# Ordering a two-layer sequence trunk by the tile scheduler's finer simulation

## The chip, the cores and the metric

The kernel runs on one core of one Trainium2 chip. The metric is the device time of one execution in microseconds. Engines are named as in the profile: PE is TensorE's matmul side, PEld its weight loads, DVE is VectorE, ACT is ScalarE, POOL is GpSimd, SP is SyncE, which here only issues DMAs.

## The reference

A sequence of 256 positions of width 1024 goes through two layers. Each layer is a half-step SwiGLU feed-forward block (FFN, inner width 2816), a mixer, and a second FFN, each with an RMS norm ahead of it and behind it and a residual addition:

```python
for i in range(DEPTH):          # 2
    x = x + 0.5 * rms_norm(swiglu(rms_norm(x, g[0]), ffn_wgu[i, 0], ffn_wd[i, 0]), g[1])
    h = rms_norm(x, g[2])
    mix = diff_rwkv_mixer(h, ...) if i % 2 == 0 else retention_mixer(h, ...)
    x = x + rms_norm(mix, g[3])
    x = x + 0.5 * rms_norm(swiglu(rms_norm(x, g[4]), ffn_wgu[i, 1], ffn_wd[i, 1]), g[5])
```

The even layer's mixer runs differential attention (4 heads) beside an RWKV-7 recurrence (8 heads of 64), both behind one input projection and ahead of one output projection. The odd layer's mixer is retention (4 heads) in matrix form. All data are float32.

## The kernel before

The 256 positions are two blocks of 128, b=0 and b=1. The plan is six sub-layers: FFN, even mixer, FFN, FFN, odd mixer, FFN. Every weight is used once by both blocks and is streamed from DRAM: `pump` (L279 to L302) issues one 512 KB DMA per half unit on SP into one of 3 `raw` buffers, then ACT rounds it to float32r (`wh`, L299) and DVE takes the rest (`wl`, L300); 8 buffers hold each of `wh` and `wl`. A product is the sum of three float32r matmuls (high by high, high by low, low by high): `proj` (L315 to L317), `outp` (L327 to L329), `proj_features` (L340 to L342). In most chunks of an FFN both blocks share one weight load in `proj_parts` (L354, L355), and `joined` (L363 and L364) adds the two halves out of PSUM on ACT and DVE, behind which come the SwiGLU steps (L528 to L535) and `outp`.

A sub-layer ends in `post` (L464 to L471: sum of squares on ACT, the inverse root on POOL, the residual addition into `x` on DVE), and the next begins with `pre` (eight transposes on PE, L418, turned into `xp` by ACT and DVE, L423 and L424). One block's hand-over from `post` to `pre` is a chain, beside which PE can only run what the other block still has.

In the even mixer, `rwkv` (one job per block, lanes 0 and 2) and `attention` (lane 1) are generators that are stepped between the units of the projections. The recurrence is solved by doubling: five levels, each a group of small matmuls (L1122), a mask on DVE (L1125), a second group (L1129), and DVE additions and transposes (L1131, L1133), each needing the one before it. PSUM has four tags of two banks: `mm`, `tp`, `ac0`, `ac1`.

All instructions are written into one block by Python; `run` (L1267) fixes the order in which the two blocks, the weight pump and the lanes are written. The order in which each engine gets them is the tile scheduler's: it simulates the program while it orders it, and hands each engine, of the instructions whose inputs and buffers are ready in the simulation, the one of highest priority. Priority is the order of writing, lifted in the hand-overs (`LIFT_PRE, LIFT_POST = 300, 100`) and in the lanes (`LIFT = (200, 600, 600)`), by that many instructions. Each engine then runs its instructions in the order given, and an instruction that waits holds up those behind it on its engine.

## Time and profile before

| | |
|---|---|
| median of 3 runs | 1206.8 us (1206.78 to 1227.89) |
| profiled execution | 1209.15 us |
| its span, first to last instruction | 1207.4 us |
| mean granted TensorE clock | 0.993 |
| PE busy | 1178.7 us |
| DVE, ACT busy | 756.6, 629.1 us |
| read from DRAM | 197.50 MB, 164 GB/s |

The span is shorter than the execution by what lies before the first and behind the last instruction, 1.75 us. Busy times are of the profiled execution; a matmul's end is modelled, so a stretch in which PE is shown busy throughout can hold short pauses.

### The profile page before, as it was taken

What the parts mean: (1) busy time and instruction counts of PE and PEld (TensorE: products, weight loads), DVE (VectorE), ACT (ScalarE), POOL (GpSimd) and SP (SyncE); (2) the same over time, 40 slices, a digit from 0 to 9 for tenths busy, and PEclk for the clock granted to TensorE, in tenths of its full rate; (3) what the DMA queues carried; (4) which work ended last, traced back from release to release, by engine and by line L of the source; (5) the groups of instructions that cost most, each with busy time, mean ns of one, the idle gap of its engine ahead of it and who ended that gap; (6) DMA issues with size and microseconds to landing.
All of it is one profiled execution on the core that took longest, in us unless ns stands there. A gap on an engine that the chain in (4) does not pass through costs nothing.

```text
span 1207.4 us, 17468 instructions
## 1 busy us (share of the span) xinstructions
PE 1178.7 (98%) x6760; PEld 966.9 (80%) x6760; DVE 756.6 (63%) x1147; ACT 629.1 (52%) x1055; POOL 39.0 (3%) x53
## 2 busy tenths in 40 slices
PE   7999999999999999999999999999999999999997
PEld 5788887788777778888878888877877777888886
DVE  5666666687644766666676656575544457666663
ACT  6554555744452465455565555565434456555552
POOL 0000000000001100000010000010000001000000
PEclk9999999999989999999999999999999999999999
DMA  8655655442141256565546556555525555556551
GB/s 278 220 189 180 204 178 177 141 132 61 37 132 45 69 178 206 186 194 188 181 159 205 190 180 192 192 192 178 178 97 175 163 167 177 194 190 192 192 189 38
DMA packets 55412, 199.70 MB, mean 165 GB/s; under 512 B 6176, under 2 KB 6432, under 8 KB 55328
## 3 DMA queue, kind: packets, MB, share of 16 engines
q1 hardware_dynamic: 54576, 196.90, 50.3%
q8 instruction: 53, 0.87, 0.3%
q0 software_dynamic: 320, 1.05, 0.3%
q10 hardware_dynamic: 432, 0.63, 0.2%
q14 instruction: 31, 0.25, 0.1%
HBM read 197.50 MB, written 1.05 MB: 164 GB/s over the span
## 4 chain that ended last, share of the span: by engine, by line
PE 84%; DMA 5%; DVE 4%; ACT 3%; issue 2%; POOL 1%; SPq 0%; DVEq 0%; POOLq 0%; ACTq 0%
PE ps L354 24%; PE ps L355 12%; PE ps L329 8%; PE ps L327 8%; PE ps L328 8%; PE ps L315 5%; PE ps L317 4%; PE ps L316 4%; DMA raw<-in_wts_dram 4%; DVE wl L300 2%; ACT wh L299 2%; PE p L1122 1%; PE p L1129 1%; PE tp L418 1%; PE yp L603 1%
## 5 line engine op out<-in xcount | busy, mean ns | idle before, releaser
L300 DVE TENSOR_TENSOR wl<-raw,wh 128x1024 fp32r<-128x1024 f32 (+1 forms) x368 | 443.1, 1207 | 251.5 <-ACT wh L299 249.3
L299 ACT CAST wh<-raw 128x1024 fp32r<-128x1024 f32 (+1 forms) x368 | 380.5, 1037 | 254.6 <-PE ps L354 73.7
L354 PE MATMUL ps<-xp,wh 128*128 128x512 f32 x1312 | 469.7, 400 | 5.7 <-DVE sgh L513 2.0
L355 PE MATMUL ps<-xp,wl 128*128 128x256 f32 x1312 | 369.0, 281 | 0.0
L354 PEld LDWEIGHTS ps<-xp,wh 128*128 128x128 f32 x1312 | 247.3, 188 | 71.1 <-DVE gate L364 10.2
L355 PEld LDWEIGHTS ps<-xp,wl 128*128 128x128 f32 x1312 | 249.3, 190 | 1.5
L327 PE MATMUL ps<-wh,hx 128*128 128x512 f32 x448 | 178.3, 398 | 0.0
L328 PE MATMUL ps<-wl,hx 128*128 128x512 f32 x448 | 177.4, 396 | 0.0
L329 PE MATMUL ps<-wh,hx 128*128 128x512 f32 x448 | 177.3, 396 | 0.0
L315 PE MATMUL ps<-wh,xp 128*128 128x512 f32 (+1 forms) x320 | 130.8, 411 | 1.8 <-ACT xp L423 1.2
L316 PE MATMUL ps<-wl,xp 128*128 128x512 f32 (+1 forms) x320 | 127.0, 399 | 0.0
L317 PE MATMUL ps<-wh,xp 128*128 128x512 f32 (+1 forms) x320 | 126.0, 398 | 0.7 <-DVE xp L424 0.5
L329 PEld LDWEIGHTS ps<-wh,hx 128*128 128x128 f32 x448 | 84.1, 188 | 20.7 <-DVE hx L376 0.3
L327 PEld LDWEIGHTS ps<-wh,hx 128*128 128x128 f32 x448 | 84.1, 188 | 20.1 <-ACT hx L375 0.4
L328 PEld LDWEIGHTS ps<-wl,hx 128*128 128x128 f32 x448 | 84.2, 188 | 18.0
L315 PEld LDWEIGHTS ps<-wh,xp 128*128 128x128 f32 x320 | 61.0, 191 | 22.1 <-ACT xp L423 7.1
L317 PEld LDWEIGHTS ps<-wh,xp 128*128 128x128 f32 x320 | 61.0, 191 | 15.8 <-DVE xp L424 2.9
L363 ACT COPY gate<-ps 128x256 f32<-128x256 f32 x74 | 27.2, 368 | 86.0 <-PE ps L355 85.9
L316 PEld LDWEIGHTS ps<-wl,xp 128*128 128x128 f32 x320 | 61.0, 191 | 12.8 <-issue 1.9
L364 DVE TENSOR_TENSOR gate<-ps,gate 128x256 f32<-128x256 f32 x74 | 31.2, 421 | 57.0 <-ACT gate L363 57.0
L363 ACT COPY h<-ps 128x256 f32<-128x256 f32 x74 | 27.1, 367 | 50.1 <-PE ps L355 50.1
L424 DVE SCALAR_TENSOR_TENSOR xp<-tp,c,xp 128x128 fp32r<-128x128 f32 x96 | 30.6, 347 | 11.9 <-ACT xp L423 10.6
(241 smaller groups left out, 959.6 us busy)
## 6 DMA issues: line engine op xcount, KB each, us to landing
raw<-in_wts_dram SPq DMA_DIRECT2D x362, 512.0 KB, 4.4
gpost<-in_rows_dram SPq DMA_DIRECT2D x6, 512.0 KB, 5.6
x<-in_x_dram SPq DMA_DIRECT2D x4, 256.0 KB, 6.2
ups<-in_ups_dram SPq DMA_DIRECT2D x1, 768.0 KB, 5.8
ce<-in_ce_dram SPq DMA_DIRECT2D x1, 644.0 KB, 8.3
lnw<-in_rows_dram POOLq DMA_DIRECT2D x2, 256.0 KB, 4.1
lnb<-in_rows_dram POOLq DMA_DIRECT2D x2, 256.0 KB, 3.7
dec<-in_co_dram SPq DMA_DIRECT2D x1, 512.0 KB, 3.5
```

Of the source, the lines that this page charges most:

```text
L299: nc.scalar.copy(out=h[:, c], in_=r[:, c])
L300: nc.vector.tensor_tensor(out=l[:, c], in0=r[:, c], in1=h[:, c].bitcast(F32), op=ALU.subtract)
L315: mm(ps[:, :width], lhsT=xh[:, kt, :], rhs=h[:, c], start=first and i == 0, stop=False)
L316: mm(ps[:, :width], lhsT=xh[:, kt, :], rhs=l[:, c], start=False, stop=False)
L317: mm(ps[:, :width], lhsT=xl[:, kt, :], rhs=h[:, c], start=False, stop=last and i == n - 1)
L327: mm(acc[n], lhsT=hh[:, t], rhs=wh[:, c], start=first and t == 0, stop=False)
L328: mm(acc[n], lhsT=hh[:, t], rhs=wl[:, c], start=False, stop=False)
L329: mm(acc[n], lhsT=hl[:, t], rhs=wh[:, c], start=False, stop=last and t == 1)
L354: mm(ps, lhsT=h[:, c], rhs=both, start=kt == 0, stop=False)
L355: mm(ps[:, :256], lhsT=l[:, c], rhs=both[:, :256], start=False, stop=kt == 7)
L363: self.nc.scalar.copy(out=o, in_=ps[:, 256:])
L364: self.nc.vector.tensor_tensor(out=o, in0=ps[:, :256], in1=o, op=ALU.add)
```

## The change

The scheduler's simulation is exchanged: with the flag, the order is found on the library's timeline simulation, which keeps the sequencers, the queues in front of the engines, the DMA queues and the semaphores as parts with times of their own, in place of the coarser one. The instructions, their operands, the number of buffers and the priorities are the same; what can differ is the order of the instructions on each engine, which buffer of a tag a tile gets, and with these the waits between the engines.

```diff
-    with tile.TileContext(nc) as tc:
+    with tile.TileContext(nc, schedule_with_timeline_sim=True) as tc:
         trunk_body(tc, io, out)
```

## Rows read from the trace of the kernel before

**Rows 1.** The page's part 1, busy time, share, instructions of each engine.

```profile
PE 1178.7 (98%) x6760; PEld 966.9 (80%) x6760; DVE 756.6 (63%) x1147; ACT 629.1 (52%) x1055; POOL 39.0 (3%) x53
```

**Rows 2.** Busy time of each engine by stretch; columns in the first row.

```profile
core 0: us, PE busy (x) PEld busy (x) DVE busy (x) ACT busy (x) POOL busy (x), PEclk, DMA share, GB/s
0.00:60.00 60.00, 50.22 (x229) 40.07 (x230) 37.60 (x72) 37.30 (x70) 1.32 (x6) 0.94 0.76 250
60.00:200.00 140.00, 139.84 (x726) 117.94 (x725) 89.55 (x110) 73.17 (x100) 0.00 (x0) 1.00 0.58 188
200.00:450.00 250.00, 243.27 (x2083) 194.10 (x2082) 162.97 (x342) 123.28 (x282) 22.87 (x25) 0.99 0.31 101
450.00:600.00 150.00, 150.00 (x787) 126.73 (x786) 95.62 (x118) 79.45 (x111) 0.00 (x0) 1.00 0.60 191
600.00:640.00 40.00, 39.61 (x181) 31.11 (x180) 28.63 (x51) 25.53 (x52) 3.12 (x4) 1.00 0.51 169
640.00:790.00 150.00, 150.00 (x787) 126.75 (x786) 95.78 (x119) 79.51 (x111) 0.00 (x0) 1.00 0.59 190
790.00:850.00 60.00, 57.92 (x278) 46.34 (x278) 40.05 (x62) 37.40 (x65) 3.06 (x4) 1.00 0.58 188
850.00:1030.00 180.00, 177.41 (x830) 141.10 (x829) 100.07 (x143) 88.22 (x144) 7.52 (x12) 1.00 0.49 158
1030.00:1190.00 160.00, 160.00 (x830) 134.69 (x829) 99.96 (x124) 82.16 (x115) 0.00 (x0) 1.00 0.55 178
1190.00:1207.40 17.40, 10.47 (x45) 8.07 (x43) 6.38 (x11) 3.12 (x8) 1.10 (x2) 0.87 0.16 60
```

**Rows 3.** What PE waited for: us in total, times, longest us.

```profile
PE tp L418 <- DMA c<-in_c_dram: 4.2, 1, 4.2
PE tp L418 <- DVE x L471: 2.4, 6, 0.6
PE ps L354 <- DVE gate L364: 2.0, 2, 1.8
```

**Rows 4.** Stretches at TensorE's lower clock and one behind; columns as above.

```profile
25.40:28.80 3.40, 3.40 (x12) 2.81 (x12) 2.69 (x3) 1.50 (x3) 0.00 (x0) 0.50 0.94 338
52.70:56.10 3.40, 3.40 (x13) 2.91 (x12) 3.00 (x4) 1.58 (x2) 0.00 (x0) 0.50 0.78 235
349.70:356.50 6.80, 6.80 (x31) 5.45 (x30) 3.06 (x6) 2.08 (x4) 2.31 (x4) 0.50 0.21 77
356.50:366.00 9.50, 9.50 (x69) 6.49 (x70) 4.41 (x6) 4.90 (x11) 1.43 (x3) 1.00 0.42 140
```

**Rows 5.** Timeline, PE's two long waits in the start; [idle before, what ended it].

```profile
25.16 0.59 PE L354 MATMUL ps<-xp,wh 128*128 128x512 f32 x1 [2.05 <-DVE sgh L513]
...
51.93 0.50 PE L354 MATMUL ps<-xp,wh 128*128 128x512 f32 x1 [1.85 <-DVE gate L364]
```

**Rows 6.** Timeline, one level of the recurrence (start, length, engine, line, operation).

```profile
255.97 1.15 PE L1122 MATMUL p<-work 64*64 64x64 f32 x32
...
257.48 0.68 PE L1129 MATMUL p<-work 64*64 64x64 f32 x16
...
258.40 0.68 PE L1129 MATMUL p<-work 64*64 64x64 f32 x16
258.76 0.79 DVE L1131 TENSOR_TENSOR work<-p,work 128x256 f32<-128x256 f32 x2
...
259.47 0.76 DVE L1133 STREAM_TRANSPOSE work<-work 128x256 f32<-128x256 f32 x2
...
260.88 1.15 PE L1122 MATMUL p<-work 64*64 64x64 f32 x32
```

**Rows 7.** Timeline, block 0's hand-over at 202 us; [idle before, what ended it].

```profile
202.55 0.40 PE L329 MATMUL ps<-wh,hx 128*128 128x512 f32 x1
203.34 0.66 PE L418 MATMUL tp<-c,x 128*128 128x128 f32 x4 [0.39 <-DVE x L471]
```

**Rows 8.** Activation table loads at L512, a group of the lines: busy us, mean ns.

```profile
L512 ACT ACT_TABLE_LOAD x2 | 2.6, 1283 | 0.6 <-issue 0.6
```

## The prediction

> **What bounds the kernel now.** I read the page's shares first. PE is shown busy for 1178.7 of 1207.4 us, DVE and ACT for 63% and 52% [rows 1]. No DMA figure comes near a bound over a whole stretch: the DMA engines' share in the long FFN stretches is 0.55 to 0.60 [rows 2]. So the kernel is bound by PE, and a new order can't take away matmuls; it can only remove or add time in which PE has nothing that it may run, and time at the lower clock.
>
> Where that time lies is read from the stretches. The inner parts of the four FFNs (60 to 200, 450 to 600, 640 to 790 and 1030 to 1190 us, together 600 us) show PE busy for 599.84 us. The even mixer with its two edges, 200 to 450, lacks 250 - 243.27 = 6.73 us; the edge at 600 to 640 lacks 0.39, that at 790 to 850 2.08, the odd mixer 2.59. The start, 0 to 60, lacks 9.78 and the end, 1190 to 1207.4, 6.93 [rows 2]. The sum is 28.7 us, the difference between the span and PE's busy time.
>
> Of this some is out of reach of any order. At the start PE waits 4.2 us for the first constants to land [rows 3]. At the end the last block's norm and its output follow the last matmul, 6.93 us. That leaves 28.7 - 4.2 - 6.93 = 17.6 us in play.
>
> The clock is the second loss. Three stretches, 3.4, 3.4 and 6.8 us long, are granted 0.50, the lower of the two levels [rows 4]. The first two stand in the start-up, each just behind one of PE's two longest waits after the first (2.05 us for DVE's `sgh`, 1.85 us for `gate`) [rows 5]. The third stands in the even mixer, in a stretch that shows PE busy throughout, so being shown busy doesn't keep the clock. With half the rate in 13.6 us, the three cost some 6.8 us by an estimate from these rows. So the most that a perfect order could give back is 17.6 + 6.8 = 24.4 us, 2.0% of 1207.
>
> **The change part by part.** Nothing is computed more or less, so every term is a wait that comes or goes. The sum is made against the profiled execution: span 1207.4 and 1.75 us around it, 1209.15, which is 2.35 above the median of 1206.8. I give the time against the median, and the differences are the same in both.
>
> *Inner FFNs, 600 us.* PE idles for 0.16 us in all of it [rows 2]. What hides everything else is that DVE is busy 64% there (95.62 of 150) and ACT 53% [rows 2], and that weights are split up to 8 half units ahead. Another order on ACT or DVE moves an eviction by at most a few casts, and there is room for that. I cost it at nothing. If the cover is gone, the price is an eviction that comes late: PE's waits for `gate` were 2.0 us in 2 cases, so about 1 us each [rows 3], and with 37 joined chunks, a wait of a tenth of that in each is 3.7 us. Bounds: 0 to +4.
>
> *The start, 60 us.* 9.78 - 4.2 = 5.6 us are in play, and the two clock losses that follow waits, 3.4 us of effect together. Bounds: -9 if all of it goes, and +9 if as much is added again; nothing in the trace shows either, and the transfers, whose share is 0.76 here and 0.94 in the first slow stretch [rows 2, 4], are not sped up by an order. I take 0.
>
> *The hand-overs.* Five edges between sub-layers, two blocks each, give ten hand-overs in which `post`, `pre` and the first product of the next sub-layer follow each other. The one at 202 us shows what the present order leaves: the last matmul ahead of it starts at 202.55 and lasts 0.40, then PE idles 0.39 us until DVE has written `x`, then the four transposes start [rows 7]. In all, PE waited 2.4 us in 6 such cases, 0.4 us each, at most 0.6 [rows 3]. This is tight: the transposes come on PE almost as soon as `x` is there, with the other block's matmuls before and after. An order that is off by one matmul, 0.40 us of record, costs or hides that much. From below, -2.4 us, all waits gone; from above, ten hand-overs at two more matmuls each, 8 us. I take one matmul each, +4 us, because the rows leave less than that to be gained.
>
> *The even mixer, 250 us.* This is where order matters, and there are 2083 matmuls in it [rows 2], most of them small. One level of the recurrence takes 4.9 us, from the L1122 group at 255.97 to the next at 260.88, and within it PE's own groups last 1.15 + 0.68 + 0.68 = 2.5 us [rows 6]. The other 2.4 us are DVE's additions and transposes, and the projections' matmuls fill them, so that PE shows no wait. Bounds: -6.7 us, all present idle time gone, and -3.4 for the clock; for the upper end see the first rival, +58. I take 0, because the row that is nearest, PE's idle share of 2.7% in this stretch [rows 2], is what the same work cost under an order from a simulation.
>
> *The odd mixer and the rest, 850 to 1030 and the two edges.* 5.1 us of idle time between them [rows 2], bounds -5 and +5, taken as 0: the same reason.
>
> *Table loads.* The FFN's Silu has ACT load a table twice, 1.283 us each [rows 8]. An order that brings the mixer's exponentials and the FFN's Silu across one another adds pairs, 2.6 us of ACT's time each, which its 48% of idle time hides outside of hand-overs. 0, at most +5 for two pairs on the path.
>
> The sum: 0 + 0 + 4 + 0 + 0 + 0 = +4, so 1206.8 + 4 = about 1211 us, +0.3%.
>
> **A rule that is weighed.** In the even mixer PE is busy for 97.3%, the weight loads for 194.1 of 250 us, 78%; in the inner FFNs it is 126.73 of 150, 84% [rows 2]. The Trainium skill (Perfetto Trace Analysis, section Identifying the Most-Contended Engine) holds that matmul busy time is a poor measure of the distance to the limit and that the busy share of weight loads is a better one. By that, the mixer would have 7 points more to give, an estimate of 17 us, and the time would be about 1190. The trace doesn't decide it, since the small groups have another ratio of load to matmul than the large ones; it counts toward the third case below.
>
> **The rivals.**
>
> *First, slower: the recurrence falls behind its filler.* A finer simulation can hold several instructions in front of an engine. If the scheduler hands PE ready projection matmuls that far ahead, a link of the recurrence that becomes ready a moment later stands behind them, whatever its priority. The filler is used up early, and the later links run with nothing beside them: then each level shows its 2.4 us outside of PE [rows 6]. Two blocks with five levels each and about seven more steps of that kind make 24 such gaps; 24 x 2.4 = 58 us if all are bare, 29 if half are. The hand-overs would suffer by the same mechanism, at the upper bound of 8 us. Half bare gives 1207 + 29 + 8 = 1244, all bare 1273. It decides for "slower" from about 24 us, that is from 10 bare gaps or, with 8 us at the hand-overs, from 7. For it: the priorities are lifted by only a few hundred instructions, and the present order leaves little idle time, so there is more to lose than to win. A thinner PE also risks the lower clock, which the stretch at 349.7 shows for just this mixer: 31 matmuls in 6.8 us there against 69 in the 9.5 us behind it [rows 4]. Against it: PE executes in this stretch what is ready in the simulation, and a simulation with more of the machine in it should leave fewer waits that it didn't foresee.
>
> *Second, no effect: the order changes nowhere that matters.* In the inner FFNs one order is nearly forced, and if the mixer's links come in the same places, the time is 1207, within 2 us. Against it: with 2083 matmuls in the mixer and several ready at any time, two simulations will hardly agree.
>
> *Third, faster: the finer simulation sees the waits that PE now has and fills them.* It would take away half to all of the 24.4 us: 1207 - 12 = 1195 to 1182. For it, the start's two waits with the clock losses behind them [rows 4, 5]. Against it, the waits at the hand-overs and the start are the ends of chains, and there must be matmuls that are ready to put there; and at the start the transfers limit.
>
> **How the numbers follow.** The forecast, a few microseconds either way (1199 to 1222), gets 0.47; no effect 0.08; the faster case 0.10; the recurrence falling behind 0.35. I count 2% (24 us) as what a measurement of this kernel can tell from no change. Over 2% faster needs all of the faster case, 0.02. Over 2% slower is nearly all of the first rival, 0.33. Within 2% is the rest, 0.65. For 8 times in 10 the range drops the better half of the faster case, below 1194, and the upper quarter of the slower one, above 1265: 1194 to 1265. The forecast's own range is 1199 to 1222.
>
> **What would show it.** Right: the four inner FFN stretches keep PE at full busy time; PE's idle time grows or shrinks by under 10 us; the waits for `x` and `xp` at the edges change by tenths. If the first rival holds: the stretch between the first recurrence group and the end of the even mixer gets longer while its early part is dense with projection matmuls, the late levels have PE waiting for L1125, L1131 and L1133, and the lower clock shows up more often there. If the third holds: the waits of 2.05 and 1.85 us in the start and the slow stretches behind them are gone. My forecast fails if ACT's or DVE's order lets evictions come late in the inner FFNs, which I cost at nothing: PE would then wait for `gate` and `h` in every chunk, and 600 us would grow as a whole.

## The result and the profile after

The changed kernel takes 1245.94 us (median of 4 runs, 1244.05 to 1247.3), the kernel before 1217.35 in the runs beside it. The ratio is 1.0285, with a 95% interval of 1.0231 to 1.0338: slower, by 0.0285 x 1217, about 35 us. The profiled execution is 1247.3 us, its span 1245.5 against 1207.4, its mean granted TensorE clock 0.976 against 0.993. The ratio leaves out runs more than 1.5% above the fastest of their kernel, so it is not the ratio of the two medians, and below such runs are only in numbers called a median or said to be of all runs.

The page's first part, the row that answers to [rows 1]:

```profile
PE 1185.2 (95%) x6760; PEld 978.0 (79%) x6760; DVE 756.5 (61%) x1147; ACT 620.9 (50%) x1055; POOL 39.3 (3%) x53
```

The counts are the same, and PE's busy time grew by 6.5 us only. Its idle time doubled: 1245.5 - 1185.2 = 60.3 us against 28.7. The busy time of each engine by stretch, in the columns of [rows 2], says where:

```profile
0.00:60.00 60.00, 49.91 (x227) 39.16 (x228) 37.02 (x70) 36.20 (x67) 1.31 (x6) 0.97 0.74 250
60.00:180.00 120.00, 120.00 (x623) 102.27 (x622) 74.68 (x92) 60.12 (x86) 0.00 (x0) 0.99 0.59 188
180.00:240.00 60.00, 50.39 (x228) 39.09 (x227) 32.42 (x60) 30.63 (x60) 3.76 (x4) 0.91 0.41 126
240.00:400.00 160.00, 156.91 (x1700) 131.10 (x1700) 108.98 (x232) 75.26 (x182) 13.60 (x15) 1.00 0.28 90
400.00:480.00 80.00, 72.66 (x347) 56.57 (x346) 48.04 (x82) 36.81 (x71) 5.88 (x6) 0.96 0.40 127
...
600.00:660.00 60.00, 53.77 (x244) 42.91 (x242) 36.49 (x62) 32.24 (x62) 3.55 (x4) 0.91 0.43 137
...
805.00:880.00 75.00, 64.77 (x287) 52.29 (x287) 42.07 (x64) 38.62 (x67) 3.48 (x4) 0.89 0.47 152
...
1020.00:1080.00 60.00, 54.19 (x240) 41.84 (x239) 37.25 (x63) 32.87 (x63) 2.20 (x4) 0.97 0.51 168
```

The inner FFNs stay full (120.00 of 120; the others are as full). The three stretches that hold the end of an FFN, 180 to 240, 600 to 660 and 805 to 880, lack 9.61, 6.23 and 10.23 us, and the two in which an FFN follows a mixer, 400 to 480 and 1020 to 1080, lack 7.34 and 5.81. These five are 39.2 of the 60.3 us, and all five are granted a lower clock than 1.00. The stretch with most of the recurrence lacks 3.09 us.

What PE waited for, to be held against [rows 3]:

```profile
PE ps L327 <- ACT hx L534: 12.8, 3, 4.9
PE ps L315 <- ACT xp L423: 6.4, 10, 2.1
PE ps L327 <- ACT hx L375: 6.3, 3, 3.0
PE tp L418 <- DVE x L471: 4.5, 4, 1.4
PE ps L354 <- DVE q L364: 4.0, 1, 4.0
```

The first row is new: three waits of `outp` for the cast at L534, the end of the SwiGLU chain of a joined chunk. The timeline of the first of them, where [rows 7] show the same edge before:

```profile
199.75 0.39 PE L329 MATMUL ps<-wh,hx 128*128 128x512 f32 x1
199.78 1.23 DVE L300 TENSOR_TENSOR wl<-raw,wh 128x1024 fp32r<-128x1024 f32 x1 [0.19 <-ACT wh L299]
...
200.92 0.42 DVE L364 TENSOR_TENSOR h<-ps,h 128x256 f32<-128x256 f32 x1
201.26 1.22 DVE L300 TENSOR_TENSOR wl<-raw,wh 128x1024 fp32r<-128x1024 f32 x1
202.39 0.68 DVE L532 TENSOR_TENSOR h<-h,gate 128x512 f32<-128x512 f32 x1
203.45 1.04 ACT L299 CAST wh<-raw 128x1024 fp32r<-128x1024 f32 x1 [2.49 <-DMA raw<-in_wts_dram]
204.40 0.61 ACT L534 CAST hx<-h 128x512 fp32r<-128x512 f32 x1
...
205.07 0.79 PE L327 MATMUL ps<-wh,hx 128*128 128x512 f32 x1 [4.93 <-ACT hx L534]
...
212.83 0.40 PE L329 MATMUL ps<-wh,hx 128*128 128x512 f32 x1
214.67 1.32 PE L418 MATMUL tp<-c,x 128*128 128x128 f32 x8 [1.44 <-DVE x L471]
```

PE starts its last ready product at 199.75 and has nothing until 205.07, while one chain runs: addition (L364), multiplication (L532), cast (L534). These three take 0.42 + 0.68 + 0.61 = 1.71 of the 4.93 us. Most of the rest is weight work that stands ahead of each link on its engine: on DVE two remainders (L300), on ACT a weight cast (L299) that itself waited for its DMA.

In the order before, the joined projections were all done earlier, and five groups of twelve output products lay behind the last of them. The last joined matmul starts at 191.47, the same cast runs at 195.17 right behind the multiplication, and output products run without a break until 202.95, so that the chain costs PE nothing:

```profile
191.47 0.28 PE L355 MATMUL ps<-xp,wl 128*128 128x256 f32 x1
...
195.17 0.62 ACT L534 CAST hx<-h 128x512 fp32r<-128x512 f32 x1 [0.23 <-DVE h L532]
```

The finer simulation had handed PE some of those groups ahead of the projections, since they were ready. Behind 205.07 the products of both blocks alternate, so both end at 213.2, and the hand-over stands bare too: block 0's eight transposes come after 1.44 us with no product left beside them, where before its first four came after 0.39 with block 1's products around them [rows 7].

The stretches at the lower clock ahead of the last 10 us, five of twelve, and the sum of the twelve, in the same columns:

```profile
203.30:210.10 6.80, 5.03 (x12) 3.97 (x13) 1.83 (x2) 1.56 (x2) 0.00 (x0) 0.50 0.72 233
216.90:220.30 3.40, 3.09 (x8) 1.94 (x8) 3.40 (x9) 1.68 (x5) 2.66 (x2) 0.51 0.80 224
404.70:408.10 3.40, 3.37 (x10) 2.89 (x11) 1.42 (x3) 1.68 (x3) 0.00 (x0) 0.50 0.00 0
462.70:466.10 3.40, 3.40 (x10) 2.54 (x9) 2.76 (x5) 1.45 (x3) 0.00 (x0) 0.50 0.77 257
...
865.50:872.30 6.80, 5.95 (x19) 5.08 (x20) 3.25 (x4) 3.32 (x4) 0.00 (x0) 0.50 0.58 190
...
sum 54.40, PE 47.57 PEld 36.16 DVE 28.95 ACT 22.77 POOL 8.04; mean PE 3.96 PEld 3.01 DVE 2.41 ACT 1.90 POOL 0.67
```

Before there were 13.6 us of these in three places [rows 4]; now 54.4 in twelve. Each of the twelve has an idle time of PE of 1.4 us or more just ahead of it or at its head: at 203.30 it is the 4.93 us above, at 216.90 the hand-over.

### The profile page after: what moved, and what is told of

It is laid out like the page before. It is cut to its first block, busy times and chain, and to the rows that moved or that the text cites. A ratio compares the mean times of both kernels' runs of the same rounds, so it can differ in the third digit from the quotient of the medians.

```text
span 1245.5 us, 17420 instructions
## 1 busy us (share of the span) xinstructions
PE 1185.2 (95%) x6760; PEld 978.0 (79%) x6760; DVE 756.5 (61%) x1147; ACT 620.9 (50%) x1055; POOL 39.3 (3%) x53
## 4 chain that ended last, share of the span: by engine, by line
PE 82%; DMA 6%; DVE 5%; ACT 4%; issue 2%; POOL 0%; SPq 0%; DVEq 0%; POOLq 0%; ACTq 0%
PE ps L354 23%; PE ps L355 12%; PE ps L327 8%; PE ps L328 8%; PE ps L329 8%; DMA raw<-in_wts_dram 6%; PE ps L317 4%; PE ps L315 4%; PE ps L316 4%; DVE wl L300 3%; ACT wh L299 2%; PE p L1122 1%; PE p L1129 1%; PE yp L603 1%; ACT junk L405 1%
## 5 line engine op out<-in xcount | busy, mean ns | idle before, releaser
L300 DVE TENSOR_TENSOR wl<-raw,wh 128x1024 fp32r<-128x1024 f32 (+1 forms) x368 | 440.2, 1206 | 309.6 <-ACT wh L299 307.0
L299 ACT CAST wh<-raw 128x1024 fp32r<-128x1024 f32 (+1 forms) x368 | 377.9, 1036 | 339.8 <-DMA raw<-in_wts_dram 148.9
L327 PE MATMUL ps<-wh,hx 128*128 128x512 f32 x448 | 182.7, 410 | 19.0 <-ACT hx L534 12.8
L328 PE MATMUL ps<-wl,hx 128*128 128x512 f32 x448 | 181.7, 406 | 0.0
L327 PEld LDWEIGHTS ps<-wh,hx 128*128 128x128 f32 x448 | 86.8, 194 | 41.3 <-ACT hx L534 14.1
L329 PEld LDWEIGHTS ps<-wh,hx 128*128 128x128 f32 x448 | 85.9, 192 | 20.7 <-DVE hx L376 0.8
L328 PEld LDWEIGHTS ps<-wl,hx 128*128 128x128 f32 x448 | 86.9, 194 | 18.5 <-issue 0.2
L315 PEld LDWEIGHTS ps<-wh,xp 128*128 128x128 f32 x320 | 62.0, 194 | 28.1 <-ACT xp L423 13.6
L424 DVE SCALAR_TENSOR_TENSOR xp<-tp,c,xp 128x128 fp32r<-128x128 f32 x96 | 31.1, 347 | 24.8 <-ACT xp L423 23.5
L423 ACT ACTIVATE xp<-tp,c 128x128 fp32r<-128x128 f32 x96 | 32.1, 363 | 21.2 <-PE tp L418 11.7
L364 DVE TENSOR_TENSOR h<-ps,h 128x256 f32<-128x256 f32 x74 | 31.0, 418 | 16.8 <-ACT h L363 16.8
```

Of the source, the lines that this page charges most:

```text
L299: nc.scalar.copy(out=h[:, c], in_=r[:, c])
L300: nc.vector.tensor_tensor(out=l[:, c], in0=r[:, c], in1=h[:, c].bitcast(F32), op=ALU.subtract)
L315: mm(ps[:, :width], lhsT=xh[:, kt, :], rhs=h[:, c], start=first and i == 0, stop=False)
L327: mm(acc[n], lhsT=hh[:, t], rhs=wh[:, c], start=first and t == 0, stop=False)
L328: mm(acc[n], lhsT=hh[:, t], rhs=wl[:, c], start=False, stop=False)
L329: mm(acc[n], lhsT=hl[:, t], rhs=wh[:, c], start=False, stop=last and t == 1)
```

## Splitting the clock from the order

Runs of one kernel differ by up to 2.8%, and nearly all of that goes with the clock. The kernel before has runs with a span of 1201.3 us at a mean granted clock of 0.999, 1209.5 at 0.990 and 1223.6 at 0.979. A least-squares fit of the span to one constant for each kernel and one common slope, over 106 runs of all 14 kernels of this study, gives 9.76 us for each 0.01 of clock, with a scatter of 1.5 us. Over all 128 runs it gives 10.96 us, and the differences below move by at most 2.8 us, that of the changed kernel to 19.0 (pe_queue_1 aside); left out of both is one run of the kernel before that took 3902.64 us at a clock of 1.0 and is not explained. The constants can be compared at equal clock; the table has their differences to the kernel before, with 95% intervals from the fit. The experiments below are read by it.

| kernel | ratio of runs, 95% interval | median clock | at equal clock, us |
|---|---|---|---|
| before | | 0.991 | 0 |
| after | 1.0285 [1.0231, 1.0338] | 0.977 | +21.0 ± 1.8 |
| pe_order_new | 1.0185 [1.0107, 1.0263] | 0.986 | +21.0 ± 1.5 |
| pe_order_old | 1.0116 [1.0025, 1.0206] | 0.989 | +15.5 ± 1.7 |
| act_dve_queue_1 | 1.0297 [1.0208, 1.0385] | 0.974 | +19.9 ± 2.0 |
| pe_queue_1 | 1.1298 [1.1223, 1.1374] | 0.931 | +102 ± 4 |
| old_ends_new | 1.0157 [1.0102, 1.0213] | 0.985 | +12.1 ± 1.3 |
| old_blocks_together | 1.0054 [1.0021, 1.0086] | 0.990 | +4.0 ± 1.0 |
| old_mixer_new | 1.016 [1.0109, 1.021] | 0.984 | +10.7 ± 1.3 |
| old_mixer_lead_new | 1.0079 [1.0035, 1.0122] | 0.988 | +6.7 ± 1.3 |
| old_recurrence_new | 1.0078 [1.0043, 1.0114] | 0.986 | +5.7 ± 1.1 |
| old_ends_mixer_new | 1.0235 [1.0178, 1.0291] | 0.985 | +19.7 ± 1.4 |
| fine_ends_written | 1.023 [1.0166, 1.0294] | 0.974 | +10.3 ± 1.6 |
| fine_ends_mixer_old | 1.0171 [1.012, 1.0222] | 0.982 | +11.3 ± 1.5 |

So the change's 35 us are about 21 of order and (0.991 - 0.977) x 976 = 14 of clock. The row of pe_queue_1 lies far outside the other kernels' clocks and is rough.

## The experiments

Most of them give an engine the order that it had under the other simulation, for all of its instructions or for some. The edit is always this one, with other lists; a dependency without a semaphore is added between neighbours of the list, and the scheduler orders the rest:

```diff
+ORDERS = [...]
+def _in_order(tc, nc):
+    by_name = {i.name: i for i in nc.cur_bb.bb.instructions}
+    info = mybir.DependencyInfo(mybir.DependencyClass.NoSync, mybir.DependencyReason.DATA)
+    for names in ORDERS:
+        seq = [by_name[n] for n in names]
+        for a, b in zip(seq, seq[1:]):
+            tc.add_manual_dep(b, a.name, info, reason="given order")
...
     with tile.TileContext(nc, schedule_with_timeline_sim=True) as tc:
         trunk_body(tc, io, out)
+        _in_order(tc, nc)
```

**First: which engine's order is it?** Theory 1 said PE's, theory 2 that of ACT and DVE, theory 3 that of the DMA queue.

pe_order_old, the flag on, PE's whole order as before:

> The finer simulation orders ACT, DVE, POOL and SP, but PE is held to its order of the kernel before. Theory 1 (PE's own order is the cause: the output products are taken early, so that nothing is left beside the end of an FFN and both blocks end together): back to 1205 to 1213 us. Theory 2 (the order on ACT and DVE is the cause: casts of weights stand ahead of the SwiGLU steps at an FFN's end): stays at 1235 us or more. Theory 3 (the order of transfers on SP): stays at 1240 or more.

Measured: 1232.3 us, span 1228.5 when profiled. It lands between the theories. The waits for L534 are gone, yet 15.5 us at equal clock remain: PE's old order beside the other engines' new ones is not the old kernel.

pe_order_new, the flag off, PE's whole order as in the changed kernel:

> The reverse: the coarser simulation orders everything but PE, which is held to its order of the changed kernel. Theory 1: 1238 to 1252 us, as the changed kernel. Theories 2 and 3: 1205 to 1220 us.

Measured: 1237.1 us, span 1233.0, 1 us under what theory 1 gave and far above the 1205 to 1220 of theories 2 and 3. The wait is back:

```profile
PE ps L327 <- ACT hx L534: 8.3, 3, 4.8
```

At equal clock it stands where the changed kernel does, 21.0 against 21.0. The order of PE is sufficient for a loss of that size, whichever simulation orders the other engines; what this kernel has over the changed one is its clock, 0.986 against 0.977.

pe_queue_1 and act_dve_queue_1 leave the flag on and make the queue that the simulation keeps in front of an engine one instruction deep, once for PE (shown), once for ACT and DVE:

```diff
+    from concourse.hw_specs import TRN2Spec
+    TRN2Spec.ENG_ISSUE_QUEUE_DEPTH = {**TRN2Spec.ENG_ISSUE_QUEUE_DEPTH, mybir.EngineType.PE: 1}
     nc = _bacc.Bacc(
```

> The finer simulation with one number of it changed: the queue of instructions that it holds in front of PE is 1 deep instead of the library's larger number. If the run-ahead of the simulated queue is what lets ready output products past matmuls of higher priority, the two blocks end apart again and the time is 1200 to 1215 us. If the finer durations or latencies are the cause, it stays at 1235 us or more.

Measured: 1372.2 us. The part on the FFN ends came, there is no wait for L534 in its trace; the time was missed by 160 us. PE's longest waits, and two stretches of its even mixer in the columns of [rows 2]:

```profile
PE tp L440 <- DVE rw L438: 17.1, 3, 7.4
PE tp L418 <- DVE x L471: 16.2, 7, 5.4
```

```profile
207.00:275.00 68.00, 51.33 (x355) 40.98 (x353) 41.39 (x103) 35.00 (x80) 3.92 (x6) 0.85 0.28 91
275.00:541.00 266.00, 235.75 (x1574) 182.93 (x1575) 104.41 (x196) 64.90 (x153) 15.03 (x16) 0.74 0.15 48
```

The recurrence is thin here and runs at a clock of 0.74. So the order depends on the depth of the simulated queue, and a queue of one is no cure.

> The same for the queues in front of ACT and DVE, PE's left alone: the two engines' orders follow the priorities, PE's order is nearly that of the changed kernel. Theory 1: 1236 to 1252 us. Theory 2: at most 1225 us, since the SwiGLU steps no longer stand behind casts that were queued ahead.

Measured: 1248.4 us, L534 waited for 13.4 us in 4 cases. That is theory 1's time, but this run did not take away what theory 2 named: at the first FFN end of its trace the cast at 201.30 still stands behind a weight cast, which waited 2.38 us for its DMA. What speaks against theory 2 is pe_order_new, which has the loss with the coarser simulation's order on ACT and DVE. The weight casts ahead of the chain's links lengthen the wait in either kernel; how short it would be without them was not tried.

**Second: which part of PE's order?** Theory 1 by then: the three FFN ends, 26.6 us by the lag of the same instructions between the two traces ahead of each end and behind it.

fine_ends_written, the flag on, `outp` of each FFN's last three chunks kept in the order of writing. All joined projections then stand ahead of the last five groups of products, and block 1 ends after block 0 (its lines are two further down):

```diff
-    def outp(self, acc, u, hT, first, last):
+    def outp(self, acc, u, hT, first, last, pin=False):
...
+                    if pin:
+                        self.tc.keep_in_program_order(i)
...
-            self.outp(acc, u, hT.pop(d), d == 0, c == NCH)
+            self.outp(acc, u, hT.pop(d), d == 0, c == NCH, c >= NCH - 2)
```

> The changed kernel (finer simulation on), but the output products of each FFN's last three chunks are kept in the order in which the code writes them, so that all joined projections stand ahead of the last five groups of them and block 1's last products stand behind block 0's. Theory 1 (the finer simulation lets TensorE take ready output products ahead of the last projection, so that the last SwiGLU chain and the hand-over to the next stage stand bare at three FFN ends; 9.7 + 7.4 + 9.5 = 26.6 us by the lag of the changed trace behind the old one): about 1219 us for a profiled span of 1245.5 (1212 to 1227), the 12.8 us of waits for hx of L534 gone, the even mixer's first transposes within 4 us of the old kernel's. Rival (the time is lost in the mixers and at the entries of the FFNs, and the ends only show it): 1238 or more.

Measured: 1238.76 us, span 1226.6 when profiled. The wait for L534 fell from 12.8 to 0.5 us, and the first hand-over needs no wait:

```profile
PE ps L328 <- ACT hx L536: 0.5, 1, 0.5
```

```profile
202.55 0.40 PE L328 MATMUL ps<-wh,hx 128*128 128x512 f32 x1
202.79 1.03 PE L420 MATMUL tp<-c,x 128*128 128x128 f32 x8
```

The median is the rival's outcome (1238 or more), the profiled span theory 1's, and the clock decides which: the profiled run had 0.982, the median is 0.974. At equal clock 21.0 - 10.3 = 10.7 us of the order's loss came back; nothing of the clock's loss did. Theory 1 was right on the place, and its 27 us, a lag that had the clock in it, are more than twice what the order there is worth.

old_ends_new, the flag off, at the three FFN ends alone the last four joined projections' matmuls (64) and the output products behind them (60) in the new order:

> The kernel before (coarse simulation), with one piece alone of the new TensorE order: at the ends of the first three FFNs the last four joined projections' matmuls and the output products behind them follow each other as the finer simulation had them; the rest is left to the coarse scheduler. Theory 1: about 27 us slower than the kernel before, span about 1234 (1226 to 1241), three waits of 4 to 5 us for hx of L534, lower-clock stretches behind each. Rival (mixers and entries): within 7 us of the kernel before.

Measured: 1228.91 us, span 1219.0; at equal clock +12.1, between theory 1 and the rival, and the same size as what fine_ends_written gave back. Of the three waits only the first is of the size expected, 4.85 us; the others are 1.71 each.

```profile
PE ps L327 <- ACT hx L534: 8.3, 3, 4.9
PE tp L418 <- DVE x L471: 5.5, 6, 1.4
```

old_blocks_together, of that piece only the last 48 output products of each end, so that the blocks end together while the projections stay ahead:

> The kernel before, with half of that piece: all joined projections stay ahead of the last output products, but the last two chunks' output products of the two blocks are interleaved as the finer simulation had them, so that both blocks end together and nothing is left to cover the hand-over of the first. If the uncovered SwiGLU chain is the larger half (the 4.9 us wait and a lower clock behind it): +2 to +4 us an end, span 1213 to 1220, no wait for hx of L534 over 1 us, a wait for x of L471 of 1 to 5 us at each end. If the joint end of the blocks is the whole of it: span 1228 or more. If neither matters: within 4 us of the kernel before.

Measured: 1217.45 us; at equal clock +4.0, 1.3 an end and so under the 2 to 4 expected. There is no wait for L534, and the hand-over waits as long as in the changed kernel:

```profile
203.31 0.40 PE L329 MATMUL ps<-wh,hx 128*128 128x512 f32 x1
205.14 1.32 PE L418 MATMUL tp<-c,x 128*128 128x128 f32 x8 [1.44 <-DVE x L471]
```

So of the ends' 12.1 us the blocks' joint end is 4.0, and the bare SwiGLU chain, with the weight casts in it, 8.1, about its three waits (8.3 us).

old_mixer_new, the flag off, PE's order new in the even mixer alone:

> The kernel before, with TensorE's order in the even mixer alone taken from the finer simulation (from the mixer's first transposes to the last product before the second FFN). My first rival in the prediction (the recurrence's links stand behind filler): 29 to 58 us slower, span 1236 or more. Theory 1 (the mixer isn't where the time goes; the changed trace passes its links 13 us faster, in part because its filler was done earlier): between 12 us faster and 6 us slower, span 1195 to 1213.

Measured: 1229.0 us, +10.7 at equal clock: outside theory 1's bounds, and below the rival's. Stretches from the mixer's first transposes to the recurrence's first link (L1100) and from there to the second FFN's transposes, in the columns of [rows 2], first of the kernel before, then of this one:

```profile
203.30:245.10 41.80, 39.45 (x208) 31.18 (x208) 29.11 (x67) 31.61 (x72) 2.56 (x3) 1.00 0.46 151
245.10:415.30 170.20, 167.93 (x1717) 136.51 (x1718) 108.93 (x229) 67.35 (x162) 17.18 (x18) 0.98 0.23 73
```

```profile
202.90:263.20 60.30, 51.46 (x266) 42.41 (x266) 34.24 (x75) 36.59 (x81) 3.54 (x4) 0.92 0.40 134
263.20:436.40 173.20, 165.62 (x1659) 136.13 (x1658) 103.05 (x215) 62.80 (x152) 15.25 (x16) 0.91 0.21 68
```

58 matmuls have moved from the second stretch into the first, products of L340 to L342 that were filler. PE idles 8.84 us in the first (2.35 before) and 7.58 in the second (2.27). Theory 1 as the whole cause fell here: put into the kernel before, the new order costs about as much in the mixer as at the ends. The changed kernel's own trace does not show that loss in the mixer. The same two stretches there:

```profile
214.70:266.60 51.90, 46.05 (x254) 36.84 (x254) 31.11 (x72) 32.95 (x76) 4.19 (x4) 0.97 0.42 133
266.60:423.60 157.00, 154.11 (x1659) 127.42 (x1658) 102.96 (x213) 62.61 (x152) 14.81 (x16) 0.99 0.24 75
```

Together they last 208.9 us, against 212.0 in the kernel before. The stages on either side are longer instead, the clock's part included, from one sub-layer's first transposes to the next's: the first FFN 210.5 after 199.1 us, the second 210.8 after 196.7.

**Third: both halves of the mixer, and both pieces together.**

old_mixer_lead_new, the flag off, only the 246 instructions from the even mixer's first transposes to the first link in the new order:

> The kernel before, with TensorE's order taken from the finer simulation only for the 246 instructions that it puts between the even mixer's first transposes and the recurrence's first link; among them are 59 of the products of L340 to L342 that the old order keeps as filler for the recurrence. From the last call: over all kernels' runs a core's span grows by 9.5 us for each 0.01 that the mean granted clock is lower, and at equal clock the changed kernel stands 21.0 us above the kernel before, old_ends_new 11.8, old_mixer_new 10.5, fine_ends_written 10.3: ends and even mixer look like two halves of it. In old_mixer_new TensorE idled 6.5 us more ahead of the first link and 5.3 us more behind it. If the loss lies in the filler being spent early: +7 to +11 us at equal clock. If it lies in the recurrence's own order (my first rival of the prediction): +0 to +4.

Measured: +6.7 at equal clock, 1.0079, both from six of its twelve runs, just under the first range; with all runs it is +6.9. The median of all twelve, 1233.37, and its trace are not used.

old_recurrence_new, the 997 from the first link on:

> The complement: the kernel before, with only the 997 instructions of the even mixer from the recurrence's first link on in the finer simulation's order. First rival of the prediction (links stand behind filler): +6 us or more at equal clock (the forecast's price was 29 to 58). Filler spent early: +0 to +4, or a gain.

Measured: 1221.44 us, +5.7, between the two ranges. PE's waits in its recurrence, two that matter:

```profile
PE tp L371 <- DVE work L1238: 3.9, 1, 3.9
PE po L1148 <- DVE gram L1138: 2.3, 1, 2.3
```

Each stands once, the longer at the recurrence's end, where its filler is used up. Neither half is the whole; spending filler early and the links' own order cost about as much, together 12.4 against the 10.7 of both at once.

fine_ends_mixer_old, the flag on, both pieces as before:

> The changed kernel (finer simulation on) with both pieces back: TensorE's order at the first three FFN ends and in the even mixer as the kernel before has it, all else left to the finer simulation. If the two pieces are the whole loss: within 5 us of the kernel before at equal clock. If the rest (the start, the FFNs' entries, the odd mixer, the order on ScalarE and VectorE) costs by itself: 8 to 15 us above it, as with TensorE held to the old order everywhere (pe_order_old stood at 15.2).

Measured: 1232.63 us, +11.3, the second of the two outcomes. Giving the mixer its old PE order back adds nothing to what fine_ends_written returned (10.3). Its waits between 200 and 500 us are at other places:

```profile
PE ps L317 <- DVE xp L424: 4.0, 3, 2.4
PE ps L315 <- ACT xp L423: 2.7, 4, 1.3
PE ps L327 <- ACT hx L375: 1.7, 1, 1.7
```

old_ends_mixer_new, the flag off, both pieces new:

> The kernel before with both pieces in the new order. If ends and mixer add: 20 to 24 us above the kernel before at equal clock, as the changed kernel. If they are one loss that shows at whichever place comes first: 10 to 14.

Measured: 1238.37 us, +19.7. The pieces alone are 12.1 + 10.7 = 22.8: they add, nearly. That the changed kernel has 21.0 does not show that its loss lies in the same places, for its mixer is no longer than before.

## Why the prediction was right and where it was wrong

The time lies inside the range 1194 to 1265, and the likeliest case did not come: it was given as 1199 to 1222. The forecast's +4 us stands against +35.

**What bounds the kernel** held. PE idles for at most 0.16 us in the inner FFNs of either trace, and what changed is idle time and clock at the edges.

**Inner FFNs, 0 (0 to +4); the start, 0 (-9 to +9); table loads, 0:** right. The start lacks 10.09 us after 9.78, with its two low-clock stretches still there, and the Silu's table loads are still two. (The price named for a late eviction, about 1 us each, is the mean of one wait of 1.85 and one of about 0.2.)

```profile
L512 ACT ACT_TABLE_LOAD x2 | 2.6, 1283 | 2.8 <-PE ps L317 2.8
```

**Hand-overs, +4 (-2.4 to +8): the step that failed.** It took an edge to be one block's `post` and `pre`, off by a matmul or two, because [rows 7] show 0.39 us of wait there. (Nor is a matmul's 0.40 us of record its price: those ahead of this hand-over start 0.23 us apart.) What hid the chains in [rows 7] was the order itself, five groups of output products kept for the end; the price if that cover goes was not asked. Three FFN ends cost 12.1 us at equal clock, shown in both directions (old_ends_new, fine_ends_written): 4.0 for the hand-over that the step had in view, half its upper bound, and 8.1 for a chain that it did not have, the last joined chunk's additions, multiplication and cast, with the weight casts between them.

**The even mixer, 0 (-6.7 to +58):** not settled for the changed kernel, whose mixer is 3 us shorter. PE's new order costs 10.7 us in it when put into the kernel before (6.7 for the lead alone, 5.7 for the recurrence alone). "What the same work cost under an order from a simulation" said nothing on another simulation's order.

**The first rival, 1244 to 1273,** names the time that came, but not by its sum, so that 1244 stands beside 1246 by luck. Its mechanism, PE handed ready work far ahead and the filler used up early, is what the ends show and, in the kernel before, the mixer; that it comes from the simulated queue, pe_queue_1 points to, where the ends' waits are gone. Its main price, 24 bare gaps of 2.4 us or half of them, is refuted: the changed kernel's recurrence waits for none of L1125, L1131 and L1133, its only waits in 266.6 to 423.6 us being

```profile
PE tp L371 <- DVE work L1238: 2.2, 1, 2.2
PE tp L998 <- DVE s L987: 0.5, 1, 0.5
```

It put 29 us on the recurrence and 8 on the hand-overs; measured in the kernel before were 5.7 and 12.1, with 6.7 for the mixer's lead.

**The clock** had terms only in bounds, 3.4 us each in the start and the mixer, and a remark in the rival. It cost 14 us, 40% of the loss. Six of the twelve low-clock stretches, 30.6 of 54.4 us, lie at the three FFN ends, so part of it follows from the failed step. But fine_ends_written, with these waits gone, has a clock of 0.974, and the three hand-overs of old_blocks_together, 1.44 us each, have a clock of 1.00 behind them; which gaps the clock's loss belongs to is not shown. The rival's sign for it, 31 matmuls in the 6.8 us at 349.7, is in part the half rate itself: the 6.7 us ahead, still at 1.00, hold 55.

**The odd mixer and the rest, 0 (-5 to +5).** These bounds are broken by the idle time where the last FFN begins (5.81 us) and by the third FFN end: 805 to 1080 us lacks 16.0 us, where 790 to 1030 lacked 4.67 [rows 2].

**The weighed rule** would have had a faster kernel, 1190. That did not come, and the share of weight loads over the span hardly moved, 79% after 80%, while the time grew by 2.85%. In the changed kernel's recurrence it is 127.42 of 157.00, 81%, after 136.51 of 170.20, 80%, and that stretch is 13 us shorter with 58 matmuls fewer; the rule's 7 points were reached in no stretch read here.

**Open.** Put into the kernel before, ends and mixer cost 19.7 us, nearly the 21.0 of the change. Taken out of the changed kernel, only the ends return anything: with ends and mixer old under the finer simulation 11.3 us remain, and with PE's whole old order 15.5. The traces say where to look. PE waits for `xp` (L423, L424; L425, L426 in fine_ends_written) for 1.7 us in the kernel before, and for 11.4, 12.8 and 14.7 in pe_order_old, fine_ends_written and fine_ends_mixer_old. The second longest of these waits in the last of them, 2.37 us at 213.72, stands behind DVE's `lp` (L939), which waited 2.69 us for its DMA while the remainders of `xp` (L424) stood behind it on DVE; the kernel before has block 0's L424 ahead of it. So an old PE order beside the finer simulation's order of the other engines has a loss of its own, much of it at these casts; no run put ACT's and DVE's order alone back, so this is read from the traces and not tested. That a smaller run-ahead between one instruction and the default would be better was not tried. No kernel here beats the one before.

## What to carry to other kernels

An edge that shows almost no wait may be held together by the order: before pricing a new order, count what independent work lies behind the last link of each chain, and price the chain bare. Price with it what other work stands ahead of the chain's links on their engines: here that was more than the links. A scheduler that takes whatever is ready can spend the filler early and show the chains at the end of a stage; pinning the last work of a stage in the order of writing gave back half of the order's loss here, and none of the clock's. A piece's cost in one order need not be its cost in the other: look for it in the changed kernel's own trace too. And read times beside the granted clock: of 35 us here 14 went with it.

## What the runs showed of the hardware that was not expected

The run-to-run spread of one kernel is nearly all granted clock: 1201.3 to 1223.6 us from 0.999 to 0.979, with 1.5 us of scatter about one slope for all kernels. Not each gap costs clock, and its length alone does not tell. In the changed kernel the waits of 1.91 and 1.95 us in the start were followed by 3.4 us at 0.50 and 0.51, while one of 3.02 us at the fourth FFN's entry was followed by none:

```profile
1074.78 0.50 PE L327 MATMUL ps<-wh,hx 128*128 128x512 f32 x1 [3.02 <-ACT hx L375]
```

```profile
1072.00:1078.00 6.00, 3.09 (x12) 2.26 (x13) 4.58 (x6) 3.94 (x6) 0.00 (x0) 1.00 0.70 210
```

In the changed kernel 0.977 is (1 - 0.977) x 976 = 22 us, 1.8% of its span. The Trainium skill (TensorE: Matmul & The Clock Gate, section Part 1: The HAM clock gate) takes the ramp's penalty as under 1% of a typical kernel's span when one models it. That is for the ramp at the start; the 1.8% here hold twelve falls behind it.

And PE's busy time is no fixed sum: with 47.57 us of it at half rate against 13.6, it should have grown by (47.57 - 13.6) / 2 = 17 us for the same matmuls, and it grew by 6.5. Records of pipelined matmuls may overlap differently in another order; I did not follow it further.
